# Trainium2: the last twenty slots of a matmul with a decayed running sum, in another order, and its last slot in two halves

## The chip, the cores and the metric

One core of a Trainium2 chip runs the whole kernel. The metric is the device time of one execution in microseconds, the median of five runs. Beside the times there is one profiled execution, from which all single durations come; its times count from the start of its span.

Engines in this text: TensorE (PE in the profile), VectorE (DVE), ScalarE (ACT), GpSimd (POOL) and SyncE (SP), which here only issues stores. PSUM is the memory that TensorE writes, in banks of 512 float32 for each of 128 partitions.

## The reference

```python
B, S, D = (16, 2048, 1024)          # x: [B, S, D], w: [D, D], decay: [D]
xw = x @ w
out[:, 0, :] = xw[:, 0, :]
for t in range(1, S):
    out[:, t, :] = decay[None, :] * out[:, t - 1, :] + xw[:, t, :]
```

So it is a matrix product, followed along time by a first-order recurrence with a factor of its own for each of the 1024 columns. All is float32; the kernel multiplies in bfloat16.

## The kernel before

**Slots.** Time is cut into 64 chunks of 512 steps (four for each of 16 batch rows), and the 1024 output columns into 8 blocks of 128, n = 0 to 7. A *slot* is one column block for one group of chunks. The groups are pairs of chunks (1024 steps) except for the last pair, whose two chunks are groups of their own. That gives 31 x 8 wide slots and 16 slots of 512 steps, 264 in all. The text counts them from the end: slot -1 is the last, -20 to -17 are the last four wide ones, -16 to -9 are the chunk before the last, -8 to -1 the last chunk. In PSUM a slot holds time along the free axis and the 128 columns on partitions, so that the recurrence is a scan along the free axis.

**What is done for a slot.** TensorE multiplies (`matmul`, L126: 8 products for each chunk) into a PSUM tile. There are three tiles `ps` of two banks each, taken in turn, and in the narrow slots n = 3 and n = 7 use a tile of one bank, `spare`. Then the slot goes one of two ways, by the attribute `paired`:

- *Plain*: VectorE scans the PSUM tile itself, out[t] = decay * out[t-1] + in[t], in `scan` (L193), into an SBUF tile `so`.
- *Paired*: the recurrence is taken two steps at a time. `pair` has ScalarE copy the PSUM tile to `xs` (L167) and form `h`, decay times its even steps (L157), and GpSimd adds that to the odd steps (L173). VectorE scans only the odd steps, with decay squared (L179), at half the length. `complete` fills in the even steps: ScalarE multiplies (L157), GpSimd adds (L207).

The paired way takes half the scan from VectorE and gives the work to ScalarE and GpSimd. `complete` also copies the last step to `keep` (L210), with which the next group of the same batch row and column block begins; `pair` puts the `keep` of the group before, or a zero, in front of `so` (L172, L170). The tiles `so` (four), `xs` (three) and `h` (four) are taken in turn.

**The way out.** `back` (L218) transposes `so` by blocks of 32 on VectorE into an outlet tile `ot`, which collects four column blocks. When the fourth is there, SyncE issues four stores (L239), one for each quarter of the partitions, in rows of 128 float32 (512 bytes): 512 KB each for a wide group, 256 KB for a narrow one. The last four slots have no outlet. There `cross` has TensorE transpose `so` by 128 x 128 into PSUM with an identity matrix (L330), four column blocks beside each other; ScalarE and VectorE copy them to SBUF (L332), and four stores of 256 KB go out in rows of 2 KB (L335). `cross` runs twice, for the first and for the second half of the 512 steps.

**What sets the order.** The order of every engine is the program order, written down: `pin` keeps it. After a slot's matmuls a list of deeds is done. In the middle of the program `usual` makes the list; the first 17 and the last 16 slots have it in `agenda`, a string of letters with slot numbers: P is `pair`, S `scan`, C `complete`, B `back`, I the identity, V `cross`. Each engine takes its own instructions from that sequence one after the other. `flips` names slots whose way (paired or plain) is turned around. Unless flipped, a slot is plain where n % 4 is 3.

```python
-16: "I P-16 B-17 S-16 C-16 C-17",
-15: "P-15",
-14: "S-15 B-18 B-16 P-14",
-13: "P-13 S-14 S-13 B-15",
...
-3: "S-3 S-4 C-4",
-2: "S-2",
-1: "S-1 V0 V1",
...
flips = (0, 1, -2, -3, -15, -8)
```

Of the kernel before, what the change touches and what calls it, by code (L numbers as in the profile page):

```python
# [9 lines left out]
FP32 = mybir.dt.float32  # L10
BF16 = mybir.dt.bfloat16
ALU = mybir.AluOpType


def _ap(ap_obj: bass.AP, new_ap, extra_offset=0):
    return dataclasses.replace(
        ap_obj,
        ap=[list(p) for p in new_ap],
        offset=ap_obj.offset + extra_offset,
    )  # L20
# [5 lines left out]
def kernel(  # L26
# [26 lines left out]
    nc = tc.nc  # L53
    pin = tc.keep_in_program_order
    B, S, D = x.shape
    assert w.shape == (D, D)

    NQ = 4
    P = 32
    CQ = D // NQ  # L60
    K = CQ // P
    M = K // 2
    TL = 512
    NJ = TL // P
    NC = S // TL
    R = K // 2
    CH = D // 2
# [3 lines left out]
    sb = ctx.enter_context(tc.tile_pool(name="sb", bufs=1))  # L71
    psp = ctx.enter_context(tc.tile_pool(name="psp", bufs=1, space=bass.MemoryType.PSUM))
# [3 lines left out]
    def ring(pool, name, count, shape, dtype=FP32):  # L76
        i = turns[name] = turns.get(name, -1) + 1
        return pool.tile(shape, dtype, name=f"{name}{i % count}")
# [10 lines left out]
    dec = const.tile([128, K], FP32, name="dec")  # L89
# [9 lines left out]
    xt_of = {}  # L99
# [24 lines left out]

    def matmul(ps, n, k, xt, t0=0, t1=TL, start=0):
        pin(nc.tensor.matmul(  # L126
            out=ps[:, t0:t1],
            lhsT=wsb[:, k, n].rearrange("p q i -> p (q i)"),
            rhs=xt[:, k // 2, k % 2, t0:t1],
            start=(k == 0 and t0 == start),  # L130
            stop=(k == K - 1),
        ))
# [3 lines left out]
    class Tile:  # L136
# [3 lines left out]
        def __init__(self, g, n, ps, outlets):  # L140
            self.b, self.t0 = chunks[g[0]]
            self.T = TL * len(g)
            self.n, self.ps, self.outlets = n, ps, outlets
            self.paired = n % R != R - 1
            if len(tiles) in flips or len(tiles) - len(slots) in flips:
                self.paired = not self.paired
            self.so = ring(sb, "so", 4, [128, 2 * TL + 2])
            self.prev = None if self.t0 == 0 else last[n]
            if self.t0 + self.T < S:
                last[n] = const.tile([128, 1], FP32, name=f"keep{n}", bufs=2)  # L150
                self.keep = last[n]
            else:
                self.keep = None

        def decayed(self, src):
            h = ring(sb, "h", 4, [128, TL])[:, 0:self.T // 2]
# [3 lines left out]
            return h  # L160

        def pair(self):
            if not self.paired:
                return
            T = self.T
            self.xs = ring(sb, "xs", 3, [128, 2 * TL])[:, 0:T]
            pin(nc.scalar.copy(out=self.xs, in_=self.ps))  # L167
            g = self.decayed(self.ps[:, 0:T:2])
            if self.prev is None:
                pin(nc.gpsimd.memset(self.so[:, 1:2], 0.0))  # L170
            else:
                pin(nc.scalar.copy(out=self.so[:, 1:2], in_=self.prev))  # L172
            pin(nc.gpsimd.tensor_tensor(  # L173
                out=self.xs[:, 1:T:2], in0=g, in1=self.xs[:, 1:T:2], op=ALU.add))

        def scan(self):
            T, n, so = self.T, self.n, self.so
            if self.paired:
                pin(nc.vector.tensor_tensor_scan(  # L179
                    out=so[:, 3:T + 2:2],  # L180
                    data0=squares[-1][:, n:n + 1].to_broadcast([128, T // 2]),
                    data1=self.xs[:, 1:T:2],
                    initial=0.0 if self.prev is None else self.prev,
                    op0=ALU.mult,
                    op1=ALU.add,
                ))
            else:
                parts = self.ps if isinstance(self.ps, tuple) else (self.ps,)
                size = T // len(parts)
                before = 0.0 if self.prev is None else self.prev  # L190
                for i, ps in enumerate(parts):
                    t = 2 + i * size
                    pin(nc.vector.tensor_tensor_scan(  # L193
                        out=so[:, t:t + size],
                        data0=dec[:, n:n + 1].to_broadcast([128, size]),
                        data1=ps,
                        initial=before,
                        op0=ALU.mult,
                        op1=ALU.add,
                    ))  # L200
                    before = so[:, t + size - 1:t + size]

        def complete(self):
            T, so = self.T, self.so
            if self.paired:
                h = self.decayed(so[:, 1:T + 1:2])
                pin(nc.gpsimd.tensor_tensor(  # L207
                    out=so[:, 2:T + 2:2], in0=h, in1=self.xs[:, 0:T:2], op=ALU.add))
            if self.keep is not None:
                pin(nc.scalar.copy(out=self.keep, in_=so[:, T + 1:T + 2]))  # L210

        def back(self, half=None):
            n, c0 = self.n, self.n % R * P
# [103 lines left out]
            out=ident, in_=ident, compare_op=ALU.not_equal, fill=1.0, base=0,  # L317
            pattern=[[-1, 128]], channel_multiplier=1))

    def cross(half):  # L320
        b, t0 = chunks[-1]
        nb = TL // 128 // 2
        pts = [ring(psp, *(("spare1", 1) if half and i else ("ps", 3)), [128, R, 128])
               for i in range(nb)]
        wides = [ring(sb, *(("ot", 4), ("xb", 3))[half], [128, NQ, R, P]) for _ in range(nb)]
        for r in (1, 0, 2, 3):
            so = tiles[r - R].so
            for i in range(nb):
                t = 2 + (half * nb + i) * 128
                pin(nc.tensor.transpose(out=pts[i][:, r], in_=so[:, t:t + 128], identity=ident))  # L330
        for i, copy in enumerate((nc.scalar.copy, nc.vector.tensor_copy)):
            pin(copy(out=wides[i].rearrange("p q r i -> p r q i"),  # L332
                     in_=pts[i].rearrange("p r (q i) -> p r q i", q=NQ)))
        for i in range(nb):
            pin(nc.sync.dma_start(  # L335
                out=_ap(out, [[D, 128], [1, CH]],
                        (b * S + t0 + (half * nb + i) * 128) * D + CH),
                in_=wides[i].rearrange("p q r i -> p (q r i)")))


    slots = [(g, n) for g in groups[:-1] for n in range(K)]
    slots += [([c], n) for c in groups[-1] for n in range(K)]
# [2 lines left out]
    def turn_and_load(c):  # L345
# [22 lines left out]
        "D": decays,  # L368
        "d": square_again,
        "I": identity,  # L370
        "V": cross,
        "L": lambda i: load(*loads.pop(0)) if loads else None,
    }
    agenda = {
# [15 lines left out]
        14: "L P14 T6 S13 C13 L Y6 L",  # L390
        15: "L S15 L S14 C14",
        16: "B13 B12 B15 B14 P16 X6",
        -16: "I P-16 B-17 S-16 C-16 C-17",
        -15: "P-15",
        -14: "S-15 B-18 B-16 P-14",
        -13: "P-13 S-14 S-13 B-15",
        -12: "P-12",
        -11: "B-13 C-15 P-11 S-12 C-13 S-11 C-14 C-12",
        -10: "P-10 B-14 C-11",
        -9: "P-9 S-9 B-12",  # L400
        -8: "S-10 P-8 S-8 B-11",
        -7: "C-10 C-8 C-9 P-7 B-9",
        -6: "P-6 B-10 S-7 C-7 B-8",
        -5: "P-5 S-6 S-5",
        -4: "C-6 B-7 B-5 P-4 B-6",
        -3: "S-3 S-4 C-4",
        -2: "S-2",
        -1: "S-1 V0 V1",
    }
    flips = (0, 1, -2, -3, -15, -8)  # L410
    later = {10: ["Y4"]}
    for c in range(5, nch):
        first = c // 2 * K
# [4 lines left out]
    def usual(s):  # L418
        paired = [t.paired for t in tiles]
        do = [f"P{s}"] if paired[s] else []  # L420
        if paired[s - 1]:
            do.append(f"S{s - 1}")
        if not paired[s]:
            do.append(f"S{s}")
        do.append(f"C{s - 1}")
        if paired[s - 2]:
            do.append(f"B{s - 2}")
        if not paired[s - 1]:
            do.append(f"B{s - 1}")
        return do + later.get(s, []) + ["L"] * (2 if len(loads) > NQ else 1)  # L430

    def perform(do):
        for deed in do:
            deeds[deed[0]](int(deed[1:] or 0))
# [3 lines left out]
    for step, (g, n) in enumerate(slots):  # L438
# [25 lines left out]
        if step < R:  # L464
            ps = heads[n] if n < 3 else tuple(spares)
        else:
            if len(g) == 2 or n % R < 3:
                ps = ring(psp, "ps", 3, [128, T])
            else:
                ps = ring(psp, "spare", 1, [128, TL])  # L470
            todo = [(k, l) for k in range(K) for l in range(len(g))]
            if step < K:
                todo.sort(key=lambda kl: kl[0] % 2)
            elif step == K:
                todo.sort(key=lambda kl: kl[1])
            for k, l in todo:
                matmul(ps[:, l * TL:(l + 1) * TL], n, k, xt_of[g[l]])
        tiles.append(Tile(g, n, ps, outlets))
        do = agenda.get(step, agenda.get(left) if left >= -2 * K else None)
        perform(usual(step) if do is None else do.split())  # L480
    assert not loads
# [1 line left out]
_INS = ['x', 'w', 'decay']  # L483
# [26 lines left out]
```

## Time and profile before

| | us |
|---|---|
| median of five runs | 910.95 |
| lowest and highest run | 910.21, 911.95 |
| the profiled execution | 911.95 |
| its span, first to last instruction | 910.2 |

| engine | busy us | share of the span |
|---|---|---|
| PE (matmul) | 895.8 | 98% |
| DVE | 826.9 | 91% |
| ACT | 686.9 | 75% |
| POOL | 663.2 | 73% |

The mean granted TensorE clock is 0.999 of full speed. DMA moved 204.49 MB at a mean of 225 GB/s. A group line of the profile gives the source line, the engine, the operation, the tiles out<-in, the shapes and the count, then the busy time, the mean length of one in ns, and the idle time before. Matmuls are pipelined: a matmul of 128x512 shows a length of 379 ns, but the next one starts 216 ns after it, so that lengths on PE are not to be added. The same holds on the other engines to a smaller degree: the next instruction can start some 0.04 to 0.1 us before the end of the one before, and sums are made from start to start.

### The profile page before, as it was taken

To read this page: it belongs to the slowest core of one execution; us is meant where nothing else is said; L and a number is where in the kernel's file an instruction comes from. 1 tells how busy PE (TensorE), PEld (TensorE's weight loads), DVE (VectorE), ACT (ScalarE), POOL (GpSimd) and SP (SyncE) were. 2 spreads that over 40 slices of the span, in tenths; PEclk is the share of its full clock that TensorE was granted. 3 is DMA by queue.
4 is the path that set the end of the run, shared out by engine and by line. 5 is a ranking of instruction groups with operands and counts; after the bars stand their busy time and mean duration, and the time that the engine had idled before them with its cause. 6 is when DMAs were issued, how large, how long until landed. Compare 5 with 4: busy or idle time off the path is not lost.

```text
span 910.2 us, 12038 instructions
## 1 busy us (share of the span) xinstructions
PE 895.8 (98%) x4179; PEld 409.4 (45%) x4179; DVE 826.9 (91%) x619; ACT 686.9 (75%) x954; POOL 663.2 (73%) x764
## 2 busy tenths in 40 slices
PE   7999999999999999999999999999999999999997
PEld 3544444444444444444444444444444444444443
DVE  3998999999999999999999999999999999999987
ACT  3787887877778778778778778777777787787763
POOL 7777978677777777677687786777777776776653
PEclk9999999999999999999999999999999999999999
DMA  9999999999999999999999999999999999999758
GB/s 163 177 220 236 218 219 240 254 252 256 253 239 251 226 234 232 222 232 230 224 234 222 229 228 228 230 230 226 231 230 223 234 232 221 229 234 204 172 129 242
DMA packets 402605, 204.49 MB, mean 225 GB/s; under 512 B 8816, under 2 KB 401776, under 8 KB 402544
## 3 DMA queue, kind: packets, MB, share of 16 engines
q1 hardware_dynamic: 265200, 134.76, 59.6%
q0 software_dynamic: 137344, 68.96, 56.8%
q8 instruction: 32, 0.52, 0.2%
q14 instruction: 29, 0.24, 0.1%
HBM read 138.42 MB, written 134.22 MB: 300 GB/s over the span
## 4 chain that ended last, share of the span: by engine, by line
PE 89%; DMA 4%; DVE 2%; POOL 2%; issue 2%; ACT 1%; DVEq 0%; ACTq 0%; POOLq 0%
PE ps L126 88%; DMA xb<-in_x_dram 3%; DMA ot<-in_w_dram 1%; POOL xb L105 1%; PE spare L126 1%; DVE so L193 1%; DVE ot L218 1%; DVE so L179 1%; POOL xs L173 0%; POOL ot L256 0%; ACT xs L167 0%; POOL so L207 0%; DVE xw L115 0%; ACT xt L123 0%; ACT h L157 0%
## 5 line engine op out<-in xcount | busy, mean ns | idle before, releaser
L126 PE MATMUL ps<-xt,wsb 128*128 128x512 bf16 (+1 forms) x4078 | 876.9, 377 | 5.8 <-DVE xt L123 2.2
L126 PEld LDWEIGHTS <-wsb 128*128 128x128 bf16 x4136 | 404.5, 98 | 486.7 <-issue 5.0
L173 POOL TENSOR_TENSOR xs<-h,xs 128x512 f32<-128x512 f32 (+1 forms) x192 | 244.8, 1275 | 195.6 <-ACT h L157 90.2
L167 ACT COPY xs<-ps 128x1024 f32<-128x1024 f32 (+1 forms) x192 | 190.9, 994 | 157.5 <-PE ps L126 155.6
L218 DVE STREAM_TRANSPOSE ot<-so 128x1024 f32<-128x1024 f32 (+1 forms) x260 | 299.9, 1191 | 0.8
L207 POOL TENSOR_TENSOR so<-h,xs 128x512 f32<-128x512 f32 (+1 forms) x192 | 243.9, 1270 | 36.4 <-ACT h L157 19.7
L123 ACT COPY xt<-xw 128x2048 bf16<-128x2048 bf16 (+1 forms) x132 | 240.7, 1825 | 9.7 <-DVE xw L115 9.7
L105 POOL DMA_DIRECT2D xb<-in_x_dram x264 | 174.0, 660 | 2.0 <-DMA ot<-in_w_dram 0.9
L157 ACT ACTIVATE h<-so,dec 128x512 f32<-128x512 f32 (+1 forms) x192 | 146.5, 763 | 36.0 <-DVE so L179 32.6
L115 DVE STREAM_TRANSPOSE xw<-xb 128x2048 f32<-128x2048 f32 (+1 forms) x70 | 147.4, 2105 | 7.2 <-DMA xb<-in_x_dram 7.0
L179 DVE TENSOR_TENSOR_SCAN so<-spare,keep,xs 128x512 f32<-128x512 f32 (+1 forms) x98 | 120.8, 1233 | 28.4 <-POOL xs L173 28.1
L179 DVE TENSOR_TENSOR_SCAN so<-spare,xs 128x512 f32<-128x512 f32 x90 | 110.0, 1223 | 31.3 <-POOL xs L173 28.4
L157 ACT ACTIVATE h<-ps,dec 128x512 f32<-128x512 f32 (+1 forms) x192 | 131.3, 684 | 0.0
L193 DVE TENSOR_TENSOR_SCAN so<-dec,keep,ps 128x1024 f32<-128x1024 f32 (+1 forms) x34 | 74.6, 2195 | 0.0
L193 DVE TENSOR_TENSOR_SCAN so<-dec,ps 128x1024 f32<-128x1024 f32 x33 | 74.5, 2260 | 0.0
L210 ACT COPY keep<-so 128x1 f32<-128x1 f32 x136 | 25.2, 187 | 0.3 <-DVE so L193 0.3
L172 ACT COPY so<-keep 128x1 f32<-128x1 f32 x98 | 18.7, 191 | 1.5 <-DVE ot L218 1.5
L126 PE MATMUL spare<-xt,wsb 128*128 128x512 bf16 (+1 forms) x58 | 13.2, 342 | 0.0
L170 POOL MEMSET so<- 128x1 f32 x94 | 10.9, 116 | 1.1 <-ACT keep L210 1.1
L256 POOL DMA_DIRECT2D ot<-in_w_dram x16 | 8.7, 542 | 3.2 <-DMA xb<-in_x_dram 1.6
L274 PE MATMUL spare<-idle 128*128 128x512 bf16 x27 | 8.2, 478 | 2.3 <-ACT idle L272 2.3
L264 ACT COPY wsb<-ot 128x512 bf16<-128x512 bf16 x7 | 4.0, 616 | 5.5 <-DMA ot<-in_w_dram 5.5
(31 smaller groups left out, 33.6 us busy)
## 6 DMA issues: line engine op xcount, KB each, us to landing
out_dram<-ot SPq DMA_DIRECT2D x248, 512.0 KB, 10.5
xb<-in_x_dram POOLq DMA_DIRECT2D x248, 256.0 KB, 7.7
out_dram<-ot SPq DMA_DIRECT2D x14, 256.0 KB, 4.2
xb<-in_x_dram POOLq DMA_DIRECT2D x16, 128.0 KB, 5.3
ot<-in_w_dram POOLq DMA_DIRECT2D x12, 128.0 KB, 5.0
ot<-in_w_dram SPq DMA_DIRECT2D x4, 128.0 KB, 4.0
out_dram<-xb SPq DMA_DIRECT2D x2, 256.0 KB
ot<-in_w_dram POOLq DMA_DIRECT2D x4, 64.0 KB, 4.8
```

The costliest lines, as they stand in the source:

```text
L105: pin(nc.gpsimd.dma_start(out=xb_of[c][quad(q), j0:j1], in_=_ap(x, [[D, P], [P * D, j1 - j0], [1, CQ]], (b * S + t0 + j0 * P) * D + q * CQ)))
L115: pin(nc.vector.transpose(out=dst.rearrange("p (m j i) -> p j m i", m=M, i=P)[:, j0:j1, m0:m1], in_=src.rearrange("p (j m c) -> p j m c", ...
L123: pin(copy(out=xt_of[c][:, m0:m1, :, j0 * P:j1 * P], in_=src))
L126: pin(nc.tensor.matmul(out=ps[:, t0:t1], lhsT=wsb[:, k, n].rearrange("p q i -> p (q i)"), rhs=xt[:, k // 2, k % 2, t0:t1], start=(k == 0 a ...
L157: pin(nc.scalar.activation(out=h, in_=src, func=mybir.ActivationFunctionType.Copy, scale=dec[:, self.n:self.n + 1]))
L167: pin(nc.scalar.copy(out=self.xs, in_=self.ps))
L173: pin(nc.gpsimd.tensor_tensor(out=self.xs[:, 1:T:2], in0=g, in1=self.xs[:, 1:T:2], op=ALU.add))
L179: pin(nc.vector.tensor_tensor_scan(out=so[:, 3:T + 2:2], data0=squares[-1][:, n:n + 1].to_broadcast([128, T // 2]), data1=self.xs[:, 1:T:2 ...
L193: pin(nc.vector.tensor_tensor_scan(out=so[:, t:t + size], data0=dec[:, n:n + 1].to_broadcast([128, size]), data1=ps, initial=before, op0=A ...
L207: pin(nc.gpsimd.tensor_tensor(out=so[:, 2:T + 2:2], in0=h, in1=self.xs[:, 0:T:2], op=ALU.add))
L210: pin(nc.scalar.copy(out=self.keep, in_=so[:, T + 1:T + 2]))
L218: pin(nc.vector.transpose(out=outlet.ot[:, :, c0:c0 + P], in_=self.so[:, 2 + t0:2 + t0 + nj * P].rearrange("p (i t) -> p i t", t=P)))
```

## The change

Three things change; everything up to the matmuls of slot -20 stays as it was.

1. **Other orders for slots -20 to -1.** `pair` and `complete` are split into their single instructions, each with a letter (p copy, g odd steps, z value in front, j GpSimd's sum; h, c, k likewise for `complete`), and 20 lists in `agenda` place them one by one. Slot -20 first does what is left of the slots before it (`rest`).
2. **Another pairing.** Slots -19, -18, -16, -11 and -6 become plain, and -15 becomes paired. Slots -8, -3 and -2 stay plain, as do -17, -13, -9, -5 and -1.
3. **The last slot in two halves of time.** Slot -1 is multiplied in two halves of 256 steps, each into its own PSUM tile (`spare` and a `ps`), so 16 matmuls of 256 columns in place of 8 of 512, and scanned in two scans of 256 (a, b). The way out is one function `ending`: the four blocks of 128 steps are transposed in the order 0, 1, then 2 and 3 together, and each block has its own PSUM tile, its copy (ScalarE, VectorE in turn) and its store right behind the copy. The SBUF tiles they are copied to are `xb`, three times, and `h`, where they were two `ot` and two `xb`.

The diff, cut to its core (the functions that only split `pair` and `complete` are left out):

```diff
     def matmul(ps, n, k, xt, t0=0, t1=TL, start=0):
         pin(nc.tensor.matmul(
-            out=ps[:, t0:t1],
+            out=ps[:, t0:t1] if ps.shape[1] >= t1 else ps,
...
+        def scan_half(self, half):
+            size = self.T // 2
+            self.run(self.ps[half], half * size, size)
...
-    def cross(half):
+    def ending(i):
         b, t0 = chunks[-1]
...
+        cross((0,), range(R))
+        cross((1,), range(R))
+        cross((2, 3), range(R - 1))
+        cross((2, 3), (R - 1,))
         for i in range(nb):
-            pin(nc.sync.dma_start(
...
+            leave(i, (nc.scalar.copy, nc.vector.tensor_copy)[i % 2])
...
-        -16: "I P-16 B-17 S-16 C-16 C-17",
-        -15: "P-15",
-        -14: "S-15 B-18 B-16 P-14",
-        -13: "P-13 S-14 S-13 B-15",
-        -12: "P-12",
-        -11: "B-13 C-15 P-11 S-12 C-13 S-11 C-14 C-12",
-        -10: "P-10 B-14 C-11",
-        -9: "P-9 S-9 B-12",
-        -8: "S-10 P-8 S-8 B-11",
-        -7: "C-10 C-8 C-9 P-7 B-9",
-        -6: "P-6 B-10 S-7 C-7 B-8",
-        -5: "P-5 S-6 S-5",
-        -4: "C-6 B-7 B-5 P-4 B-6",
-        -3: "S-3 S-4 C-4",
-        -2: "S-2",
-        -1: "S-1 V0 V1",
+        -20: "z-20",
+        -19: "p-20 g-20",
+        -18: "j-20 S-19 S-20 k-19 B-19",
+        -17: "h-20 k-20 c-20 S-18 B-20 k-18",
+        -16: "I S-17",
+        -15: "z-15 B-18 k-17",
+        -14: "p-15 g-15 B-17 z-14 j-15",
+        -13: "p-14 S-16 g-14 j-14 S-15 k-16",
+        -12: "S-13 h-15 k-15 c-15 S-14 k-13",
+        -11: "p-12 B-13 h-14 B-15 g-12 c-14 k-14 B-16",
+        -10: "j-12 B-14 z-12 S-12 z-10 S-11",
+        -9: "p-10 k-12 g-10 h-12 B-11 j-10 k-11",
+        -8: "S-9 c-12 S-10 k-9",
+        -7: "z-7 B-12 h-10 k-10 B-9 c-10 S-8",
+        -6: "p-7 g-7 B-10 j-7 B-8",
+        -5: "S-7 S-6 h-7 c-7",
+        -4: "z-4 S-5 B-7",
+        -3: "p-4 B-6 g-4 B-5 j-4",
+        -2: "S-3 S-4",
+        -1: "S-2 h-4 c-4 a-1 b-1 V",
     }
-    flips = (0, 1, -2, -3, -15, -8)
+    flips = (0, 1, -19, -18, -16, -11, -8, -6, -3, -2)
...
+            if left == -1:
+                ps = tuple(both[:, t:t + TL // 2] for t, both in zip(
+                    (0, TL // 2), (ps, ring(psp, "ps", 3, [128, TL]))))
+                for t, half in zip((0, TL // 2), ps):
+                    for k in range(K):
+                        matmul(half, n, k, xt_of[g[0]], t, t + TL // 2, t)
+                todo = []
```

## Prediction

> **What bounds the kernel now.** I read the chain of waits first, as shares of the whole span:
>
> ```profile
> PE 89%; DMA 4%; DVE 2%; POOL 2%; issue 2%; ACT 1%; DVEq 0%; ACTq 0%; POOLq 0%
> ```
>
> TensorE carries nearly everything, and the diff leaves its first 244 slots alone: in the two built programs the instructions of every engine, with the semaphore counts they wait for, are the same up to about 863 us. So the whole difference must come from the last 47 us. The chain in order of time shows that stretch (start, length, what):
>
> ```profile
> 894.82 5.18 PE ps L126 x24
> 900.00 1.74 PE spare L126 x8
> ...
> 901.76 1.29 DVE so L193
> ...
> 903.10 0.55 PE ps L330 x3
> ...
> 904.45 0.69 DVE xb L332
> ```
>
> TensorE never waits until 901.74; four slots take 6.91 us here (894.82 to 901.74), so a 512-wide slot takes 1.73. Then come the last scan, the transposes and the last copy, done at 905.14. The span ends 5 us later, so I read what happens in between. SyncE's timeline (start, length) has the stores:
>
> ```profile
> 882.32 5.79 SPq L239 DMA_DIRECT2D out_dram<-ot  x4
> ...
> 904.08 1.30 SPq L335 DMA_DIRECT2D out_dram<-ot  x2
> 905.47 1.08 SPq L335 DMA_DIRECT2D out_dram<-xb  x2
> ```
>
> and the table by stretch says whether the DMA engines keep up (last two columns: their busy share, GB/s):
>
> ```profile
> 877.00:883.00 6.00, 6.00 (x29) 2.70 (x28) 6.00 (x8) 1.98 (x7) 2.70 (x6) 1.00 0.06 16
> 883.00:887.00 4.00, 4.00 (x20) 1.86 (x19) 4.00 (x6) 3.05 (x12) 2.15 (x3) 1.00 0.79 179
> ...
> 891.00:895.00 4.00, 4.00 (x20) 1.84 (x19) 3.71 (x6) 3.00 (x10) 2.24 (x4) 1.00 0.98 262
> 895.00:899.00 4.00, 4.00 (x21) 1.77 (x19) 3.99 (x6) 1.57 (x4) 2.15 (x3) 1.00 1.02 266
> 899.00:903.00 4.00, 3.60 (x19) 1.75 (x17) 3.93 (x4) 0.53 (x1) 0.73 (x1) 1.00 0.98 232
> ...
> 907.00:908.00 1.00, 0.00 (x0) 0.00 (x0) 0.00 (x0) 0.00 (x0) 0.00 (x0) 0.96 1.01 385
> ```
>
> This is the reading that decides the case. The DMA engines idle until 883 (share 0.06), then are nearly always busy to the end; in slices of 0.75 us the last bytes move in the one from 908.5 (I take 908.9). They start late because the 2 MB of slots -20 to -17 are issued at 882.32, and then 6.29 MB follow without a gap: 5.24 MB in rows of 512 B, at 179 GB/s in the first 4 us and 230 to 266 later, then the last 1.05 MB, in rows of 2 KB, at 385. The stretch 905 to 906 has 299 GB/s, a mixture of 236 (903 to 905) and 385 that puts the change at 905.6. The end is the end of a queue of stores that started late; the compute chain only feeds its last items.
>
> Why 882.32? VectorE's timeline:
>
> ```profile
> 874.83 2.26 DVE L193 TENSOR_TENSOR_SCAN so<-dec,ps 128x1024 f32<-128x1024 f32 x1
> 877.01 2.35 DVE L218 STREAM_TRANSPOSE ot<-so 128x1024 f32<-128x1024 f32 x2
> 879.28 0.71 DVE L179 TENSOR_TENSOR_SCAN so<-spare,keep,xs 128x256 f32<-128x256 f32 x1
> 879.90 1.25 DVE L193 TENSOR_TENSOR_SCAN so<-dec,keep,ps 128x512 f32<-128x512 f32 x1
> 881.07 1.81 DVE L218 STREAM_TRANSPOSE ot<-so 128x1024 f32<-128x1024 f32 x2
> ```
>
> The fourth transpose of that outlet (slot -18) stands behind the scans of -16 and -15, and ends at 882.29.
>
> **Part 1: new orders and pairing.** I walk down each engine's new order: an instruction starts when its engine is free (start to start, from the rows) and its input is there (0.03 to 0.1 us after the producer's end, as in the rows). The same walk over the old order gives the trace's starts from 863 on within 0.12 us. Start to start: scan of 1024 in one go 2.18 (874.83 to 877.01), transpose 1.13 (two from 877.01 to 879.28), paired scan of 1024 1.14, scan of 512 1.16, paired 0.63, transpose of 512 0.60. Slots end on TensorE at 901.74 minus 16 x 1.73 = 874.10 (-17), 870.65 (-18), 867.2 (-19).
>
> VectorE's new order: scan -19 at 867.25, scan -20 at 869.43 (its GpSimd sum is done at 868.3, after ScalarE's copy of 1.91 that now goes first), transpose -19 at 870.57, scan -18 at 871.70, transpose -20 at 873.88, scan -17 at 875.01 (end 877.27), transposes -18 and -17 at 877.18 and 878.31. The outlet is full at 879.52, the store issued at 879.55: 2.77 earlier. The next three outlets, walked the same way, are full at 885.5, 892.8 and 898.2 (now 887.8, 893.5, 898.7).
>
> Price: slots -19, -18, -16, -11, -6 change from paired to plain, -15 the other way: VectorE gains 2 x 1.04 + 2 x 0.53 = 3.1 us of scans. Its idle time in the same stretch is 3.8 us (2.3 and 0.9 waiting for GpSimd before 870.3 and 873.7, the rest small): it just fits. ScalarE and GpSimd lose work and have gaps of 1 to 3 us, so theirs costs nothing. The cover is thin in one place: TensorE's slot -14 reuses the bank pair that scan -17 frees at 877.27, and would start at 877.38; with 0.05 of signalling 0.06 is left, and 0.08 for slot -12 behind scan -16. Late VectorE there means TensorE late one to one; 0 to 0.1 us, I take 0.
>
> **Part 2: last slot in halves.** TensorE: 16 matmuls of 128x256 for 8 of 128x512. The program has such matmuls at its start: the table counts 39 that touch 23 to 27 us, each 0.272 long, so they are (4.0 + 0.27) / 39 = 0.109 apart, and 16 take 1.74 against 1.73: nothing. Scans: with -3 at 898.33 instead of 898.65, then -4, -2, the first half starts at 901.29. A plain scan of 256 has no row; between the paired 256 (0.71) and half of the 512 (0.63) I take 0.71. The second half waits for the first: in the program's start the second half of a scan in two parts begins 0.12 after the first's end (36.02 + 1.18 = 37.20, then 37.30). So 902.00, 902.11, 902.82, against 903.04 now: 0.2 gained. Splitting alone costs 2 x 0.71 - 1.25 + 0.11 = 0.28; the earlier start pays for it.
>
> [...]
>
> **Part 3: blocks leave one by one.** Block 0 needs only the first half: its last transpose starts at 902.05, ScalarE's copy runs 902.37 to 902.96 (0.59, as now), issue at 902.98 against 904.08. Block 1 on VectorE: 902.8 to 903.5. Blocks 2 and 3: 903.6 to 904.2 and 903.7 to 904.4. SyncE's issues last 0.42, 0.77, 0.55, 0.44 now with 0.05 between; kept, they start at 902.98, 903.52, 904.34, 904.93: 1.1 to 1.2 earlier. The four new buffers are free for long, so nothing waits for them.
>
> **The sum, on the queue.** First bytes move 0.9 after an issue (issue at 882.32, traffic from 883.2). The stream starts 2.77 earlier and stays full until its last outlet of 1.05 MB. That one used to stand in the queue: full at 898.7, moved from about 901.4 (905.6 less 1.05 MB at 250). What lies ahead of it is now gone at 901.4 - 2.77 = 898.6, and it can begin at 898.2 + 0.05 + 0.9 = 899.1: the queue just runs dry. Its bytes then take 3.9 to 4.5 us at 232 to 266 GB/s, and 5.3 if a dry queue starts as slowly as at 883 (4 us at 179, the rest at 250): gone at 903.0 to 904.4, where I take 903.7 (now 905.6). The last four stores can begin at 902.98 + 0.9 = 903.9 and take 1.05 / 0.385 = 2.7: last bytes at 906.6, the lower limit; behind 904.4 it would be 907.1. I take 906.9, against 908.9: 2.0 us. The last issue alone (904.93 + 0.9 + a quarter of 2.7) allows 906.5. The profiled execution took 911.95 for a span of 910.2, 1.75 around it, and was the highest of five; it would become 909.95, and on the median, 910.95, I forecast 908.9.
>
> [...] The rows say 230 to 266 GB/s against 385 for 2 KB. [...]
>
> **Rivals.** (1) *The stores stay the bound at a lower rate.* Filling the gap does not help if stores that meet an empty queue go at 179 GB/s throughout: the last outlet takes 5.9 instead of 4.2, is gone at 905.0, and the end is 907.7: 1.2 gained, 909.75. That is within 0.2% (1.8 us, about what a measurement of this kernel can tell from no change). For it: the first row of the stream. Against: share 0.98 to 1.02 from 891 on, with only one or two stores ahead.
> (2) *TensorE starts to wait* (slower): VectorE, filled up, is late at scan -17 or -16, and slot -14 or -12 finds its bank taken. Price: the lateness, one to one; from 0.06 us on it costs, from 2.0 it eats the gain, from 3.8 it is slower by 0.2%: with 4.2 late, 908.9 + 4.2 = 913.1. Against: every input of the scans before it has 1 us of margin (868.3 against 869.43).
> (3) *The change does not move the store*: excluded for the order (the transpose of -17 stands ahead of scan -16 in the built program), open only if the outlet's buffer is still being stored; the old order met no such wait at 871.5. Then the queue stays where it is and only its last items come sooner, 0.2 to 0.4: 910.6.
>
> **How the numbers follow.** Forecast 0.70; rival 1 0.18; rival 2 0.06; rival 3 0.06. The forecast's own range is a gain of 2.3 to 1.7, 908.65 to 909.25; the median of five runs that lie from 910.2 to 911.95 adds some 0.6 on both sides, so it starts at 907.9. Above it goes to 910.3, past rival 1. Faster by over 0.2% means under 909.1, which takes most of the forecast, but not its upper third: 0.58. Same, with that third and rivals 1 and 3: 0.36. Slower: 0.06.
>
> **What would show it.** Right: first store of the 2 MB near 879.6, 512-byte rows gone by 904, last store issued near 905, TensorE without a gap until 901.8. Wrong: an idle line of TensorE at L126 in 877 to 881 (rival 2); DMA under 200 GB/s in 899 to 904 and the last four stores still queued behind it (rival 1); the first store still near 882 (rival 3).

## The result: 1.3 us faster, where 2.0 were forecast

The changed kernel takes 909.67 us (median of 30 runs, 908.56 to 912.13) against 910.98 (51 runs) before: ratio 0.9985, 95% interval 0.998 to 0.999. That is 1.3 us faster, in the upper part of the range given (907.9 to 910.3); the forecast was 908.9. The profiled execution took 909.87 for a span of 907.8.

The chain of waits, as shares of the span, still belongs to TensorE, and more so than before (89%):

```profile
PE 93%; ACT 2%; DMA 2%; POOL 1%; DVE 1%; issue 1%; DVEq 0%; ACTq 0%; POOLq 0%
```

Two executions differ at their start, before anything that the change touches. TensorE's unbroken work began 0.57 us earlier in the profile after than in the one before (92.91, 93.49) and had the same length. Times are therefore counted below from the moment at which TensorE's last product ends, called **E**: 901.74 before, 901.17 after. Part of the chain of waits after (start, length, what); E is the start of the first transposes, L367:

```profile
core 0 of [0], span 907.8 us
896.83 2.59 PE ps L126 x12
899.42 0.87 PE spare L126 x8
900.30 0.87 PE ps L126 x8
901.17 0.74 PE spare L367 x4
...
903.26 0.69 DVE h L371
```

The two halves of the last slot take 1.74 together, as one slot did, and TensorE has no gap. The span ends 6.6 after E; before, it ended 8.4 after E. VectorE's timeline after:

```profile
874.47 2.25 DVE L216 TENSOR_TENSOR_SCAN so<-dec,ps 128x1024 f32<-128x1024 f32 x1
876.64 2.33 DVE L253 STREAM_TRANSPOSE ot<-so 128x1024 f32<-128x1024 f32 x2
878.90 1.24 DVE L216 TENSOR_TENSOR_SCAN so<-dec,keep,ps 128x512 f32<-128x512 f32 x1
...
900.80 0.72 DVE L216 TENSOR_TENSOR_SCAN so<-dec,keep,spare 128x256 f32<-128x256 f32 x1
901.62 0.75 DVE L216 TENSOR_TENSOR_SCAN so<-dec,so,ps 128x256 f32<-128x256 f32 x1
```

Both last transposes of the 2 MB outlet stand in a row ahead of the scan of slot -16 and end at 878.97, where the fourth ended at 882.29 before. The last two lines are the half scans. SyncE's timeline has what follows from it, the first three of that outlet's stores, the outlet of slots -8 to -5, and the last four stores:

```profile
879.01 3.10 SPq L274 DMA_DIRECT2D out_dram<-ot  x3
...
897.67 3.15 SPq L274 DMA_DIRECT2D out_dram<-ot  x4
902.56 1.53 SPq L373 DMA_DIRECT2D out_dram<-xb  x3
904.18 0.41 SPq L373 DMA_DIRECT2D out_dram<-h  x1
```

The first store is issued 22.16 before E instead of 19.42, the first of the last four 1.39 behind E instead of 2.34. The table by stretch (last three columns: granted clock, DMA share, GB/s):

```profile
877.00:883.00 6.00, 6.00 (x29) 2.73 (x28) 6.00 (x7) 3.82 (x11) 2.21 (x3) 1.00 0.43 96
...
891.00:895.00 4.00, 4.00 (x21) 1.82 (x19) 4.00 (x6) 1.40 (x4) 1.48 (x2) 1.00 1.01 265
895.00:899.00 4.00, 4.00 (x20) 1.81 (x19) 3.86 (x6) 0.96 (x2) 0.74 (x1) 1.00 0.85 208
899.00:903.00 4.00, 4.00 (x34) 3.28 (x32) 3.88 (x6) 1.11 (x2) 0.74 (x1) 1.00 0.97 234
903.00:905.00 2.00, 0.22 (x2) 0.00 (x0) 0.77 (x2) 0.59 (x1) 0.00 (x0) 1.00 0.88 314
905.00:906.00 1.00, 0.00 (x0) 0.00 (x0) 0.00 (x0) 0.00 (x0) 0.00 (x0) 1.00 1.02 383
```

The queue is busy from 880 on and has a hole in 895 to 899, which it did not have before: by the packet records, 111 GB/s in the microsecond from 898 and 164 in the one from 899, then 251. The prediction's "just runs dry" can be seen there.

### The profile page after: what moved, and what is told of

The parts are those of the page before. It is cut to its first block, busy times and chain, and to the rows that moved or that the text cites. A ratio compares the mean times of both kernels' runs of the same rounds, so it can differ in the third digit from the quotient of the medians.

```text
span 907.8 us, 12011 instructions
## 1 busy us (share of the span) xinstructions
PE 896.1 (99%) x4187; PEld 410.2 (45%) x4187; DVE 830.0 (91%) x620; ACT 680.3 (75%) x940; POOL 655.3 (72%) x754
## 4 chain that ended last, share of the span: by engine, by line
PE 93%; ACT 2%; DMA 2%; POOL 1%; DVE 1%; issue 1%; DVEq 0%; ACTq 0%; POOLq 0%
PE ps L126 92%; DMA xb<-in_x_dram 1%; ACT xt L123 1%; DVE so L216 1%; PE spare L126 1%; POOL ot L291 1%; DMA ot<-in_w_dram 1%; ACT xs L178 1%; ACT h L164 0%; POOL xs L191 0%; POOL xb L105 0%; DVE ot L253 0%; POOL so L241 0%; DVE so L196 0%; PE spare L367 0%
## 5 line engine op out<-in xcount | busy, mean ns | idle before, releaser
L191 POOL TENSOR_TENSOR xs<-h,xs 128x512 f32<-128x512 f32 (+1 forms) x188 | 240.6, 1280 | 200.7 <-ACT h L164 96.4
L178 ACT COPY xs<-ps 128x1024 f32<-128x1024 f32 (+1 forms) x188 | 187.8, 999 | 156.5 <-PE ps L126 154.7
L241 POOL TENSOR_TENSOR so<-h,xs 128x512 f32<-128x512 f32 (+1 forms) x188 | 239.8, 1276 | 38.5 <-ACT h L164 21.7
L164 ACT ACTIVATE h<-so,dec 128x512 f32<-128x512 f32 (+1 forms) x188 | 144.3, 768 | 29.9 <-DVE so L196 26.5
L196 DVE TENSOR_TENSOR_SCAN so<-spare,xs 128x512 f32<-128x512 f32 x88 | 107.6, 1222 | 27.6 <-POOL xs L191 24.8
L164 ACT ACTIVATE h<-ps,dec 128x512 f32<-128x512 f32 (+1 forms) x188 | 129.1, 687 | 0.0
L216 DVE TENSOR_TENSOR_SCAN so<-dec,ps 128x1024 f32<-128x1024 f32 x35 | 79.0, 2260 | 0.6 <-ACT h L164 0.6
L216 DVE TENSOR_TENSOR_SCAN so<-dec,keep,ps 128x1024 f32<-128x1024 f32 (+1 forms) x36 | 77.2, 2143 | 0.1
```

What stands on the lines that cost most here:

```text
L164: pin(nc.scalar.activation(out=h, in_=src, func=mybir.ActivationFunctionType.Copy, scale=dec[:, self.n:self.n + 1]))
L191: pin(nc.gpsimd.tensor_tensor(out=odds, in0=self.g, in1=odds, op=ALU.add))
L196: pin(nc.vector.tensor_tensor_scan(out=so[:, 3:T + 2:2], data0=squares[-1][:, n:n + 1].to_broadcast([128, T // 2]), data1=self.xs[:, 1:T:2 ...
L216: pin(nc.vector.tensor_tensor_scan(out=so[:, t + 2:t + 2 + size], data0=dec[:, n:n + 1].to_broadcast([128, size]), data1=ps, initial=befor ...
L241: pin(nc.gpsimd.tensor_tensor(out=self.so[:, 2:T + 2:2], in0=self.h, in1=self.xs[:, 0:T:2], op=ALU.add))
```

## The experiments

The table gathers all runs. "First" is the issue of the first of the last four stores, "rows" the last byte of the 512-byte rows, "bytes" the last byte of all, "span" the end of the span, each in us after E, good to 0.02, from one profile each. "Outside" is the median, over the executions of that kernel, of the time of an execution less its span (for the kernel before, the range of 107 executions). The last column is the median against the kernel before on the same chip.

| run | first | rows | bytes | span | outside | median, us |
|---|---|---|---|---|---|---|
| before | 2.34 | 4.60 | 7.18 | 8.43 | 1.73 to 1.86 | |
| the change | 1.39 | 2.46 | 5.35 | 6.62 | 2.09 | -1.31 |
| e0_again | 1.39 | 2.41 | 5.23 | 6.50 | 2.09 | -1.44 |
| e1_order | 2.36 | 2.44 | 6.10 | 7.36 | 1.81 | -1.07 |
| e2_tail | 2.01 | 4.81 | 7.39 | 8.64 | 1.77 | +0.07 |
| e3_back18 | 2.35 | 2.92 | 6.11 | 7.38 | 1.77 | -1.27 |
| e9_back18_tail | 1.70 | 3.34 | 5.92 | 7.17 | 1.84 | -1.23 |
| e7_whole | 2.35 | 2.48 | 6.10 | 7.36 | 2.08 | -0.87 |
| e4_less_after | 1.39 | none | 5.67 | 7.26 | 2.10 | -1.08 |
| e6_late17 | 1.39 | 2.30 | 5.13 | 6.39 | 1.83 | -0.89 |
| e10_pad16 | 1.39 | 2.61 | 5.39 | 6.67 | 1.80 | -0.95 |
| e11_pad64 | 1.39 | 2.48 | 5.37 | 6.65 | 1.75 | -1.93 |
| e12_before_pad41 | 2.35 | 4.91 | 7.50 | 8.76 | 1.77 | +1.20 |
| e13_pad64_again | 1.39 | 2.55 | 5.44 | 6.72 | 1.79 | -1.71 |

The five profiles with the last 47 us of the change (the change, e0_again and three of the pads) have spans that end 6.50 to 6.72 after E, the two with those of the kernel before 8.43 and 8.76 after it. So a difference of 0.2 to 0.3 between two single profiles shows nothing by itself. The 95% interval of a median's ratio reaches 0.8 to 1.0 us to each side in the experiments.

**e0_again: the change, unaltered**

> The changed kernel itself once more, beside the kernel before on the same chip. The profile pair gave a tail (last product of TensorE to the last landing) of 7.51 before and 5.70 after, 1.81 less, while the medians differ by 1.31. Theory Q (the tail is what changed, and the rest is the scatter of the front, which began 0.57 us earlier in one profile than in the other): the tail is again 5.6 to 5.8, whatever the front is, and the medians differ by 1.2 to 2.0. Rival F (a part of the gain is lost outside the tail, for instance TensorE waiting in some executions): the tail varies by 0.5 or more, or TensorE's unbroken stretch of 785.8 us becomes longer.

The tail repeats: last landing 5.59 after E, span end 6.50. Ratio 0.9984 (0.9975 to 0.9993). So the tail, counted to the end of the span, gives 1.81 and 1.93, and the two signs that F named are absent: the tails differ by 0.12, and TensorE takes 808.25 us from its start at 92.91 to E, as in the first pair (808.25 and 808.26). But what F says in general did happen in another place: the time outside the span is 2.05 to 2.12 in eight of ten executions, while all 107 executions of the kernel before that ran beside the experiments lie between 1.73 and 1.86. Here 0.3 us of the gain go, which neither theory had named.

**e1_order: parts 1 and 2 alone**

The branch for the halves is taken out, and V is `cross` as before.

```diff
-        -1: "S-2 h-4 c-4 a-1 b-1 V",
+        -1: "S-2 h-4 c-4 S-1 V0 V1",
```

> Parts 1 and 2 of the change alone (orders and pairing); the last slot is multiplied, scanned, transposed and stored as before. Theory Q (the store queue ends the run, and its start decides): the 2 MB outlet's store starts 2.8 us earlier, so the queue no longer stands behind the last four stores, which are issued as before, the last one 4.4 us after TensorE's last product; then 0.9 to its first bytes and 0.7 for its 256 KB: the tail goes from 7.5 to 6.2, 1.2 to 1.3 us gained, and the last four stores' issues are now the bound. Rival I (the issues of the last four stores decided already before): nothing gained, 0 to 0.1. Rival S (slow start of a dry queue): 0.5 to 0.9.

Tail 7.36, 1.07 less than before; ratio 0.999 (0.9981 to 0.9999). I falls. In size the gain lies between S (0.5 to 0.9) and Q (1.2 to 1.3); what decides for Q is that the queue is empty when the last four stores come, so that a slow start further ahead no longer counts. The stretches show an idle queue ahead of the last four stores:

```profile
903.00:904.00 1.00, 0.30 (x3) 0.06 (x1) 0.82 (x2) 0.58 (x1) 0.00 (x0) 1.00 0.19 70
904.00:905.00 1.00, 0.00 (x0) 0.00 (x0) 0.03 (x1) 0.00 (x0) 0.00 (x0) 1.00 1.01 379
```

One thing in Q was off: not the last of the four issues counts but the first. It is at 902.96, the bytes of the four flow from 903.81 to 906.70 almost without a break, and the three other stores are issued in time for that.

**e2_tail: the halves alone**

On the orders and the pairing of before, with the half products and `ending` of the change. The last slot's two scans stay in one deed:

```diff
-        -1: "S-1 V0 V1",
+        -1: "S-1 V",
```

> Part 3 with the halves alone: the last slot in halves and its blocks one by one, behind the orders and the pairing of before, so the 2 MB outlet starts at 882.3 as before. Theory Q: the last four stores are issued some 0.9 to 1.0 earlier (last one about 905.1 on the clock of before) but find the queue full until 905.6; the tail ends when the queue does, 0 to 0.3 us gained. Rival I: the gain is that of the issues, 0.9 to 1.1.

Ratio 0.9998 (0.9989 to 1.0007); the tail is 0.2 longer. The first of the last four is issued 0.33 earlier, but the rows of 512 bytes keep the queue until 4.81. SyncE's timeline:

```profile
903.24 2.29 SPq L338 DMA_DIRECT2D out_dram<-xb  x3
905.62 0.60 SPq L338 DMA_DIRECT2D out_dram<-h  x1
```

Part 3 alone brings nothing, as theory Q says. But the issues did not come 0.9 to 1.0 earlier, as expected: the last is at 4.39 after E, for 4.37 before, though its copy ended at 904.24. So this run does not test I; e1_order and e3_back18 do. The issues themselves took longer behind the full queue: of the last four the first two took 0.77 and 0.83, against 0.36 and 0.35 in the change.

**e3_back18: one transpose moved**

```diff
-        -16: "I P-16 B-17 S-16 C-16 C-17",
+        -16: "I P-16 B-17 B-18 S-16 C-16 C-17",
...
-        -14: "S-15 B-18 B-16 P-14",
+        -14: "S-15 B-16 P-14",
```

> The kernel before with one deed moved: the transpose of slot -18 goes from behind the scans of -16 and -15 to right behind the transpose of -17. The 2 MB outlet is then full at 880.5 instead of 882.3, 1.8 earlier; the following outlets are full at 888.5, 893.9 and 898.7, later by 0.7, 0.4 and 0; the last four stores are issued as before (last at 906.1). Theory Q: the queue ends ahead of the last stores, and their issues become the bound: 906.1 + 0.9 + 0.7 = 907.7 against 908.9: 1.0 to 1.2 gained, nearly the whole gain of part 1, without new pairing. Rival P (what counts is VectorE's relief or its order as a whole, not that store): 0 to 0.2 gained. Rival S (outlets that come later leave holes in the queue): about 0.5.

Ratio 0.9987 (0.9978 to 0.9996), 1.27 faster; tail 1.05 shorter. VectorE's timeline has the three transposes in a row, SyncE's the earlier store, and the last stores not earlier against E (903.95 - 901.60 = 2.35):

```profile
876.88 3.47 DVE L218 STREAM_TRANSPOSE ot<-so 128x1024 f32<-128x1024 f32 x3
```

```profile
880.37 5.79 SPq L239 DMA_DIRECT2D out_dram<-ot  x4
...
898.69 3.14 SPq L239 DMA_DIRECT2D out_dram<-ot  x4
903.95 0.85 SPq L335 DMA_DIRECT2D out_dram<-ot  x2
904.89 0.89 SPq L335 DMA_DIRECT2D out_dram<-xb  x2
```

Theory Q: the start of that store is what held the end, and 1.81 us earlier (882.32 - 901.74 against 880.37 - 901.60) was enough, where the whole change gives 2.74. Rival P falls: the new pairing is not needed for this part. The last of the four is issued at 905.38, 3.78 after E for 4.37 before, since the issues take 0.36 to 0.40 now. These 0.59 are too little for I: the last byte comes 1.07 earlier.

**e9_back18_tail: the moved transpose and the halves**

The edits of e2_tail and e3_back18 together.

> The kernel before with the one moved transpose of slot -18 and the last slot in halves with its blocks one by one: the change without its new pairing and without the rest of its orders. Theory G (the end is the later of two things, the last byte of the 512-byte rows and the first of the last four stores plus 1.0, and 2.73 on top for 1.05 MB at 385 GB/s): the 512-byte rows end 2.9 after TensorE's last product, as with the moved transpose alone, the first of the last four stores is issued 1.55 after it; 2.9 + 2.73 = 5.6 against 7.18 before and 5.34 with the change: a gain of 1.5, or 0.3 short of the change. Rival P (the new pairing is needed for the gain of the halves): no better than the moved transpose alone, 1.1. The time outside the span, 2.05 to 2.07 in the two profiles of the change and 1.74 to 1.75 in the four others, is read too.

Ratio 0.9987 (0.9978 to 0.9996). The tail is 1.26 shorter than before: 0.2 more than the moved transpose alone, which one pair of profiles can't tell from nothing, and less than G's 1.5. So P, which had 1.1, does not fall: on the change's orders and pairing the halves shorten the tail by 0.74 (7.36 in e1_order, 6.62), and there the 512-byte rows end at 2.46, here at 3.34. The rows of 512 bytes were gone at 3.34 where I had put 2.9, and G with the measured rows gives 3.34 + 2.73 = 6.07 for a measured 5.92. In the medians it is not told apart from e3_back18 nor from the change.

**e7_whole: the change with the last slot undivided**

```diff
-        -1: "S-2 h-4 c-4 a-1 b-1 V",
+        -1: "S-2 h-4 c-4 S-1 V",
```

> The change with the last slot undivided: one product tile, one scan of 512, but the blocks still leave one by one. The first of the last four stores is issued 2.2 after TensorE's last product instead of 1.4. Theory G: 2.2 + 1.0 + 2.73 = 5.95 against 5.34 with the change: 0.6 slower than the change, 1.2 faster than before. Rival L (the last issue decides, which would be 0.6 to 0.8 later): the same size, but with the transfers of the four stores apart from each other instead of in one stretch of 2.7. Rival Q0 (the 512-byte rows alone decide): no difference to the change.

Ratio 0.9988 (0.9979 to 0.9997), 0.44 to 0.57 less gain than the change. First issue at 2.35, bytes at 6.10: G, which from 2.35 gives 6.08. Q0 falls by the tail; the medians, with overlapping intervals, do not tell it. L falls too: the bytes of the four stores flow in one stretch of 2.89 (903.13 to 906.02), and the last issue, at 3.98 after E, is 0.21 later than in e1_order (3.77) for the same last byte. The profile says 0.74 for the split: the two half scans with the wait between took 1.57 (900.80 to 902.37), 0.28 more than the whole one in e7_whole (1.29), but what is behind the first half started 0.96 earlier.

**e4_less_after: the store ahead of the last four taken out**

The outlet of slots -8 to -5 is not stored, so that 1.05 MB of the output are missing.

> The change without the store of the outlet of slots -8 to -5 (1.05 MB in 512-byte rows are left out of the output; the outlet is still filled). Nothing then stands ahead of the last four stores. Theory G: they begin 1.0 after the first is issued, 2.4 after TensorE's last product, and end at 5.1 instead of 5.34: only 0.2 faster than the change, which stands where both limits meet. Rival Q1 (the 512-byte rows are still the bound by a lot): 0.6 or more faster.

Ratio 0.9993 (0.9984 to 1.0001): not faster than the change. The queue is empty before the last four stores:

```profile
899.00:903.00 4.00, 3.22 (x27) 2.52 (x25) 3.65 (x5) 1.45 (x3) 0.74 (x1) 1.00 0.14 54
903.00:904.00 1.00, 0.00 (x0) 0.00 (x0) 0.00 (x0) 0.00 (x0) 0.00 (x0) 1.00 1.05 381
904.00:905.00 1.00, 0.00 (x0) 0.00 (x0) 0.00 (x0) 0.00 (x0) 0.00 (x0) 1.00 1.03 385
```

Q1 falls: after the change the 512-byte rows are not the bound by a lot. The last four stores begin 0.85 after the first issue and go at 381 to 385 GB/s even into an empty queue. Fifteen of the sixteen parts of the last store land by 5.48 after E, as in the change; one lands at 6.10 (in the change 5.70). That one makes the 5.67, where G had 5.1; why it lags is open.

**e6_late17: VectorE made late for slot -14**

```diff
-        -16: "I S-17",
-        -15: "z-15 B-18 k-17",
+        -16: "I B-18 S-17",
+        -15: "z-15 k-17",
```

> The change with VectorE's transpose of slot -18 put ahead of the scan of slot -17 instead of behind it: scan -17 ends 1.13 later, the outlet of 2 MB is full 0.1 later. Theory T (the cover of TensorE's slot -14 is 0.06, as the prediction had it): TensorE waits 1.07 there, everything behind moves by it, and the run is 1.0 to 1.1 slower than the change, with an unchanged time after TensorE's last product. Rival H (there is more room than the walk says): TensorE waits less than 0.5 or not at all, and the run is 0 to 0.5 slower.

TensorE's timeline shows the wait that the prediction's second rival priced:

```profile
872.73 3.40 PE L126 MATMUL ps<-xt,wsb 128*128 128x512 bf16 x15
877.06 1.89 PE L126 MATMUL ps<-xt,wsb 128*128 128x512 bf16 x8 [0.93 <-DVE so L216]
```

The fifteenth product starts 14 x 0.216 after 872.73, at 875.75; the next would follow at 875.97 and starts at 877.06: 1.09 late, where 1.07 was walked. So the cover was as thin as stated (T), and lateness there is paid one to one. In the medians it cost 0.4 to 0.55 (ratio 0.9991, 0.9982 to 1.0), which is in H's range and not T's 1.0 to 1.1. The time outside the span, 1.83 in place of 2.09, which T had left out, gives some 0.26 of the difference; the tail got 0.1 to 0.2 shorter, no more than the scatter of the tails, and the rest is within the intervals.

**e10_pad16, e11_pad64, e12_before_pad41, e13_pad64_again: the time outside the span**

```diff
     pin(nc.scalar.copy(out=idle[:, 0:1], in_=idle[:, 1:2]))
+    pad = const.tile([128, 16], BF16, name="pad")
+    for i in range(16):
+        pin(nc.scalar.copy(out=pad[:, i:i + 1], in_=idle[:, 1:2]))
```

Shown is the edit with 16 copies; the others have 64, 41 and 64.

> The change with 16 copies of one element per partition on ScalarE more, put at its start, where it is idle from 2.2 to 6.9 us; nothing else. What is asked is the time outside the span: 2.04 to 2.23 in nearly all executions of the change, 1.73 to 1.86 in all of the kernel before, and of the built programs those with 2.1 have 1209 instructions on ScalarE, those with 1.8 have 1207, 1208 and 1231 to 1234. Theory A (it hangs on the length of ScalarE's program, by where its end falls): with 1225 it is 1.75 to 1.85, and the run 0.25 to 0.3 faster than the change, 1.6 to 1.7 faster than before. Rival B (it belongs to what the change does in its last microseconds, whatever the length): 2.05 to 2.1 again, and no difference to the change.

> The change with 64 such copies on ScalarE, 1273 instructions. They take 6 us and may delay the start by 1 to 2 us, which lies in the span; only the time outside it is read. Theory A64 (the end's place within blocks of 64 instructions decides): 2.05 to 2.1 as with 1209. Theory A128 (blocks of 128, or another size): 1.75 to 1.85. Rival B: 2.05 to 2.1.

> The kernel before with 41 such copies on ScalarE, 1273 instructions instead of 1232. Theory A64: the time outside the span goes from 1.75 to 2.05 to 2.1, with no other part of the change in it. Theory A128 and rival B: 1.73 to 1.86 as before.

> The change with 64 copies on ScalarE at its start, once more and with more executions, beside the kernel before: the eight executions so far gave 909.06, 1.9 below the kernel before, with a time outside the span of 1.73 to 1.79 in seven of eight and a median span of 907.2. Theory A (the time outside is 0.3 shorter and everything else as in the change, whose spans have medians of 907.35 and 907.5): median 909.1 to 909.3, 1.6 to 1.8 below the kernel before. Rival C (the spans scatter by the start, and the eight were a lucky draw): the time outside is 1.75 again, but the median span is 907.6 or more and the run 909.4 or slower, not to be told from the change.

With 16 copies that nothing waits for, the time outside is 1.76 to 1.81 in eight of eleven executions, with 64 copies 1.73 to 1.79 in seven of eight: B falls, the 0.3 do not belong to what the change does at its end. The kernel before with 1273 instructions on ScalarE stays at 1.75 to 1.85, and so does the change with 1273: A64 falls too. The three programs with 1209 instructions there (the change, e7_whole and e4_less_after; the profiles count two fewer of every program) have 2.1, the others, with 1207, 1208, 1225, 1231 to 1234 and 1273, have medians of 1.75 to 1.84. That is a coincidence of numbers, not a shown cause. The medians hide that single executions differ: five of eleven of e9_back18_tail and four of eleven of e6_late17 have 1.97 or more.

In time, the 0.3 came back with 64 copies: 909.06 and 908.90 (ratios 0.9977, 0.9967 to 0.9987, and 0.998, 0.9971 to 0.9989), the lowest of all, on tails like the change's; C falls, with a median span of 907.1 where it asked for 907.6 or more. They beat the kernel before; against the change (0.998 to 0.999) the intervals overlap. With 16 copies it did not come back: 910.04 (0.9981 to 0.9999), since its spans had a median of 908.0 against 907.35 and 907.5 of the change, with the same tail. And e12_before_pad41 was 1.2 slower than the kernel before (ratio 1.0014, 1.0003 to 1.0024), far more than its tail, 0.3 longer, explains. By the tails these two differences would lie ahead of E, but no profile shows where: that of e12 is of the fastest of its executions and has an earlier E (900.53) than the kernel before. They stay open.

## Why the prediction was right, and where it was off

**The bound: right.** The store queue ended the run, and it ended late because of where one transpose stood. Moving that alone made the tail 1.05 shorter, of the 1.81 and 1.93 of the whole change (e3_back18); splitting the last slot without it made it no shorter (e2_tail). In the medians (1.27 faster, against 1.31 and 1.44) the one move can't be told from the whole change, which pays 0.3 outside the span. Had the 512-byte rows gone at the 385 GB/s of those of 2 KB, their 5.24 MB would have taken 13.6 us in place of the 23.1 from 883.2 to 906.3 (an estimate, 5.24 / 0.385); then no queue would have stood there, and e3_back18, whose first issue is unmoved and whose last came 0.59 earlier, could have gained 0.59 at most. The measurement decides against that: in the stretches read, of two microseconds or more from 883 to the first of the last four stores and with a DMA share of 0.93 or more, the 512-byte rows went at 225 to 272 GB/s, and those of 2 KB behind them, in stretches of one or two microseconds, at 377 to 393. In the profiles before and after, stretches of two microseconds taken every half microsecond show 277 at most for the 512-byte rows. The stores also differ in the partitions that they read, 32 for the outlets and 128 for the last four; no run tells that from the length of the rows.

**Part 1: right to 0.05.** Store 2.74 earlier against E (2.77 predicted), the outlet of -8 to -5 issued at 897.67, which is 898.24 on the clock of before (898.25). TensorE did not wait; e6_late17 confirms the thin cover.

**Part 2: right in its costs, 0.1 late in its instants.** Sixteen half products took 1.74, the second half scan began 0.10 after the first's end, and the split cost 1.57 - 1.29 = 0.28, as walked. On the clock of before the first half scan began at 901.37 and the second ended at 902.94, for 901.29 and 902.82: 0.1 gained, not 0.2.

**Part 3: right in its instants, wrong in one reason.** On the clock of before the last four stores were issued at 903.13, 903.67, 904.33 and 904.75, for 902.98, 903.52, 904.34 and 904.93. The first two are 0.15 late; the lengths of the issues, kept from before (0.42 to 0.77), shrank to 0.33 to 0.41, now that the queue ahead of them was nearly empty (the 512-byte rows were gone 2.46 after E instead of 4.60).

**The queue's sum: 0.2 too much.** The last outlet's rows were gone at 904.2 on the clock of before, for 903.7 taken; they stayed within the 903.0 to 904.4 given. By the same measure those of the kernel before were gone at 906.3; the prediction's 905.6 was an instant by mean rates, while the first rows of 2 KB already moved at 905.06. Rival 1's slow start is real but short: 111 and 164 GB/s for two microseconds, then 251. The last bytes came at 907.1 instead of 906.9. The tail gained 1.81 in the first pair of profiles and 1.93 in the second, for 2.0.

**The term that was mis-sized: what lies around the span.** The sum carried 1.75 over from the profile before. It is 2.09 in the changed kernel, in nearly every execution. 1.81 to 1.93 less 0.3 gives 1.5 to 1.6; measured were 1.31 and 1.44, whose intervals reach to 1.8 and 2.3. What remains is within the scatter of the start: E lies between 899.88 and 901.74 in these profiles. Why the term grew is open.

**The rivals.** Rival 2 did not occur, but its price was shown; rival 3 is excluded by the store's time. Rival 1's number, 909.75, was near the result for another reason. The result lies outside the forecast's own range (908.65 to 909.25) and over the 909.1 of "faster", which had 0.58; it is in the case "same", which had 0.36. It lies in the wide range thanks to the 0.6 that was added for scatter, not to the sum.

**What sets the end now.** This is theory G, drawn from the first runs and put on record before e9_back18_tail, e7_whole and e4_less_after. The last byte comes at the later of two instants, the last byte of the 512-byte rows and the first of the last four issues plus 1.0, plus 2.73 for 1.05 MB at 385 GB/s. In e1_order and e7_whole the bytes began 0.85 after that issue and flowed for 2.89, together 3.74, where the sum has 3.73. The sum agrees within 0.16 with every row of the table but e4_less_after (for e1_order 6.09 for 6.10, for the change 5.19 for 5.35). After the change both instants nearly coincide, 2.46 and 2.39: by this sum, to better one alone brings next to nothing. In e4_less_after, where one of them is gone, nothing was gained, though its late part leaves that run no clean test.

## What to carry to other kernels

When transfers end the run, look for the instruction that fills the buffer of the first large store, and ask what stands ahead of it on its engine: one reordered transpose gave over half of what the whole rewrite took off the tail here, and in the median time the two can't be told apart. Before an end is shortened, ask which of its limits is reached next: to split the last slot was worth nothing while the queue stood ahead of it. A difference of 0.2% needs the span split into start, stretch and end: here E lay between 899.88 and 901.74 in the profiles, the span ended 6.50 to 6.72 after it with the same last 47 us, and TensorE's stretch from 92.91 or 93.49 to E differed by 0.01 in three of them.

## What was not expected of the hardware

The time outside the span differs from one built program to the next, for a reason that stays open: 1.73 to 1.86 in 107 executions of the kernel before, 2.04 and more in 41 of the changed one, and back at 1.73 to 1.82 in eighteen of nineteen with 64 copies on ScalarE in addition. Each issue of the last four stores took 0.33 to 0.44 on SyncE where the queue ahead was empty or nearly so (512-byte rows gone 3.34 after E at the latest), and 0.42 to 0.83 for the same 256 KB where it was full (the kernel before, e2_tail and e12_before_pad41, rows gone 4.60 to 4.91 after E).
